# A decoder step on one core: scores before the next head's queries, sums of choices one head later, and picking and putting in an order written by hand

## Chip, cores and metric

The kernel runs on one core of a Trainium2 chip. The metric is the device time in microseconds of one execution. Before the change three runs gave a median of 2760.44 us (2749.78 to 2764.14).

The core's engines work side by side, each through its own instructions in a fixed order: PE multiplies matrices (PEld loads its weights), DVE and ACT work on vectors, POOL issues the gathers and some vector work, SP issues the plain DMAs.

## The reference, cut to what matters

The reference is one step of a hybrid decoder: a projection, a recurrent head group and an attention head group, an output projection with a layer norm, and then a mixer of experts with a second layer norm. The change touches only the mixer. For each of 256 prompt tokens and 32 sample tokens it scores 8 heads x 2 x 128 keys, takes the 16 best of each half, the 16 best sums of those, and so 128 experts of 16384 for each token; each expert is a row of `peer_u` and a row of `peer_v`, 2048 wide.

```python
def peer_ffn(x, wq, subkeys, u_tab, v_tab):
    q = (xt @ wq).reshape(n, P_HEADS, 2, P_DKEY // 2)
    s = jnp.einsum('nhcd,hckd->nhck', q, subkeys).astype(jnp.float32)
    hv, hix = lax.top_k(s, P_TOPK)
    cand = (hv[:, :, 0, :, None] + hv[:, :, 1, None, :]).reshape(n, P_HEADS, P_TOPK * P_TOPK)
    cand_e = (hix[:, :, 0, :, None] * N_KEYS + hix[:, :, 1, None, :]).reshape(n, P_HEADS, P_TOPK * P_TOPK)
    tv, tpos = lax.top_k(cand, P_TOPK)
    expert = jnp.take_along_axis(cand_e, tpos, axis=-1)
    gate = jax.nn.softmax(tv, axis=-1).astype(x.dtype)
    ...
        h = jax.nn.gelu(jnp.einsum('cd,chkd->chk', xb, u_tab[eb]), approximate=False)
        return jnp.einsum('chk,chkd->cd', gb * h, v_tab[eb])
```

## The kernel before

The text of the kernel is traced and then scheduled: a scheduler puts each engine's instructions into an order by a simulated timeline, with the place in the text as priority. So the order in the text is not the order on the engine. `tc.issue_after(ins)` puts what its block traces behind `ins` on the engine of `ins`; `tc.keep_in_program_order(ins)`, used in the change, keeps `ins` in the order of the text. Memory comes in pools (`Pool`), with `bufs` buffers in turn for each name; a tile that takes the place of an earlier one, in the same ring or in a pool that was closed, waits until the earlier one's last user is done.

The sample tokens' choices and their products with `peer_u` are done earlier, beside attention (`sample_chain`). For the 256 prompt tokens (t = 0, 1, 128 each) the mixer has four stages.

**Queries and choices** (L1698 to L1721). For each head h, two queries of 128 columns are computed from `peer_wq` (16 matmuls of 128x256 each, L1707) and copied to QP. In the next pass of the loop `choose` (L1280) scores both tokens' halves (L1286) against the keys, copies them to S (L1295, two buffers), takes 16 of 128 twice in each half on DVE (`top16`, L1272), adds 54 candidate pairs (L1306), takes 16 of these, marks their places in `hit` (L1314, DVE), multiplies by the experts' numbers (L1316, POOL), sums (L1317, DVE) and writes the row numbers to GI (L1318). Then two `dot`s follow: a dot is a gather by POOL (L422) of half an expert's row for each of 128 tokens (512 KB, tag `rows`, NRW = 4 buffers) and one DVE instruction (L1678) that multiplies it by the token's x and sums. There are 256 dots. `gates` (L1320) makes the softmax of the 128 values. All these tiles, TV with the gates' values among them, lie in pool `kq`, which closes before the next stage.

**Dense product** (L1727 to L1752). The other half of all 16384 rows of `peer_u` isn't gathered: 128 blocks of 128 rows are loaded, transposed on PE (L1735), split into a high part (ACT, L1564) and a low part (DVE `ul`, L1565), and multiplied with all tokens in three matmuls a piece (L1740); the result goes into AW (L1742), an array of 128 KB a partition that lies on memory of earlier pools. A dot or two is issued after each block, and when 128 are done, `table(0)` (L1681) transposes the row numbers, gates and dots of t = 0 into TB.

**Picking and putting** (L1765 to L1849, 64 steps of four tokens). `pick` builds one-hot marks of both halves of the expert numbers (`oo`, L1768, DVE, four buffers), transposes one half (L1772), copies it (`oT`, L1774, ACT) and multiplies with AW (`px`, L1777) to pick each token's row of products. `activate` multiplies by the other mark and sums (`xj`, L1789), adds the dots, applies gelu and the gate, and scales the marks (L1799). `put` multiplies the two marks (`pa`, L1805) and copies the result over AW (L1806): AW now holds the weights of all experts. The other dots run within the first 32 steps. Beside them `smp` (L1815) gathers the sample tokens' rows of `peer_v` (two of 512 KB for each of 32 slots, the same `rows` buffers) and adds them with eight matmul records a slot in bank fs (L1822). After the steps the sample's norm (L1862 to L1866) is done and stored.

**Last product** (L1869 to L1931). 128 blocks of 1536 columns of `peer_v` are loaded (three buffers: two in pool `vr`, one in pool `vp`), split, and multiplied with AW (L1915); the other 512 columns are gathered and added (L1890). Then the second norm.

Of the kernel before, what the change touches and what calls it, by code (L numbers as in the profile page):

```python
# [50 lines left out]
NDW = 2  # L51
# [3 lines left out]
NRW = 4  # L55
# [93 lines left out]
def hybrid_decode_step(ctx: ExitStack, tc: tile.TileContext, a, outs, dbg=None):  # L149
# [1130 lines left out]
    def choose(t, h, pool, QP, SKT, TV, tag):  # L1280


        pb = bank(tag)
        for c in range(2):
            if t < 2:
                pe.matmul(pb[:, 128 * c:128 * c + 128], QP[:, 2 * h + c, P * t:P * t + P], SKT[:, 2 * h + c, :],  # L1286
                          start=True, stop=True)
            else:
                for g in range(4):
                    k = 2 * (2 * g + h) + c  # L1290
                    pe.matmul(pb[32 * g:32 * g + 32, 128 * c:128 * c + 128], QP[:, k, :], SKT[:, k, :],
                              start=True, stop=True)
        nb_ = 2 if t < 2 else 1
        S = pool([P, 2, P], "S", bufs=nb_)
        sc.copy(S.rearrange("p a b -> p (a b)"), pb[:, :256])  # L1295
        HV, HI, HF = (pool([P, 2, 16], nm, ty, bufs=nb_) for nm, ty in (("HV", F32), ("HI", U32), ("HF", F32)))
        for c in range(2):
            top16(S[:, c, :], HV[:, c, :], HI[:, c, :])
        gp.tensor_copy(HF, HI)
        gp.tensor_scalar(HF[:, 0], HF[:, 0], 128.0, None, op0=OP.mult)  # L1300

        CV, CE = (pool([P, NCAND], nm, bufs=nb_) for nm in ("CV", "CE"))
        for dst, src, en in ((CV, HV, ve), (CE, HF, gp)):
            o = 0
            for i0, ni, w in CAND:
                en.tensor_tensor(dst[:, o:o + ni * w].rearrange("p (i j) -> p i j", i=ni),  # L1306
                                 src[:, 0, i0:i0 + ni, None].to_broadcast([P, ni, w]),
                                 src[:, 1, None, :w].to_broadcast([P, ni, w]), OP.add)
                o += ni * w
        TI, TF, EF = (pool([P, 16], nm, ty, bufs=nb_) for nm, ty in (("TI", U32), ("TF", F32), ("EF", F32)))  # L1310
        hit = pool([P, 16, NCAND], "hit", bufs=nb_)
        top16(CV, TV[:, h, :], TI)
        ve.tensor_copy(TF, TI)
        ve.tensor_tensor(hit, iota[:, None, :NCAND].to_broadcast([P, 16, NCAND]),  # L1314
                         TF[:, :, None].to_broadcast([P, 16, NCAND]), OP.is_equal)
        gp.tensor_tensor(hit, hit, CE[:, None, :].to_broadcast([P, 16, NCAND]), OP.mult)  # L1316
        ve.tensor_reduce(EF, hit, AX.X, OP.add)  # L1317
        return ve.tensor_scalar(GI[t][:, 16 * h:16 * h + 16], EF, 2.0, None, op0=OP.mult)  # L1318
# [57 lines left out]
    def sample_chain(cx):  # L1376
# [77 lines left out]
        for h in range(2):  # L1454
            choose(2, h, cx, QPs, SKT, TV, "ss")
            yield 1
# [197 lines left out]
    HD = [up([P, P], f"hd{t}") for t in range(2)]  # L1654
    dp, kq = Pool("dp", "left"), Pool("kq", "left")
    XHd, XLd = dp([P, 8, NPR], "XHd", F32R), dp([P, 8, NPR], "XLd", F32R)
    TV = [kq([P, 8, 16], f"TV{t}") for t in range(2)]
# [14 lines left out]
    def dot(n=1, upto=2 * P):  # L1672

        for i in range(got[1], min(got[1] + n, upto)):
            t, s_ = dots[i]
            fetch(min(i + NRW, upto))
            r_, h_ = rows_.pop(i), HD[t][:, s_:s_ + 1]
            ve.scalar_tensor_tensor(r_, r_, 1.0, X1a[t], op0=OP.mult, op1=OP.mult, accum_out=h_)  # L1678
            got[1] = i + 1

    def table(t):  # L1681

        pb = bank("pb")
        for q, (op_, v_) in enumerate(((OP.logical_shift_right, 8), (OP.bitwise_and, 255))):
            ii, iff = up([P, P], "ii", I32), up([P, P], "iff", bufs=2)
            ve.tensor_scalar(ii, GI[t], v_, None, op0=op_)
            if q:
                ve.tensor_scalar(iff, ii, 0.5, None, op0=OP.mult)
            else:
                ve.tensor_copy(iff, ii)  # L1690
            pe.transpose(pb[:, 128 * q:128 * q + 128], iff, ident)
# [7 lines left out]
    subkeys([kw_([P, 8, P], "wraw", bufs=WB) for _ in range(2)], SKT, "pb")  # L1699
    for h in range(9):  # L1700
        for c in (2 * h, 2 * h + 1) if h < 8 else ():
            pb = bank("pj")
            for o in range(0, 16, 8):
                w = kw_([P, 8, P], "wraw", bufs=WB)
                sy.dma_start(w, w_q[:, 128 * c:128 * c + 128].rearrange("(k p) c -> p k c", p=P)[:, o:o + 8])
                for k in range(8):
                    pe.matmul(pb[:, :NPR], w[:, k, :], XT[:, o + k, :], start=(o + k == 0), stop=(o + k == 15))  # L1707
            sc.copy(QP[:, c, :], pb[:, :NPR])
# [14 lines left out]
    banks(pt=3, ph=2, pb=3)  # L1723
    aw = Pool("aw", "right")
    AW = aw([P, 2, NPR, 64], "AW")

    def dense(i1):  # L1727
# [4 lines left out]
        for q in range(2):  # L1732
# [5 lines left out]
            for e in range(4):  # L1738
                for wi, xi in ((wh, XHd), (wh, XLd), (wl, XHd)):
                    pe.matmul(ph[:, :NPR], wi[:, e, :], xi[:, 4 * q + e, :NPR],  # L1740
                              start=(q == 0 and e == 0 and wi is wh and xi is XHd), stop=(q == 1 and e == 3 and wi is wl))
        sc.copy(AW[:, i1 // 64, :, i1 % 64], ph[:, :NPR])  # L1742
        return lo_

    tabled = []
    for i1 in range(P):
        lo_ = dense(i1)
# [3 lines left out]
        if got[1] >= P and i1 and not tabled:  # L1751
            tabled.append(table(0))  # L1752
# [10 lines left out]
    hot, prod, act = {}, {}, {}  # L1763

    def pick(u):  # L1765
        tk = slice(4 * u, 4 * u + 4)
        oo = hot[u] = x4p([P, 2, 4, P], "oo", bufs=4)
        i_ = ve.tensor_tensor(oo, iota[:, None, None, :].to_broadcast([P, 2, 4, P]),  # L1768
                              TB[:, 0:2, tk, None].to_broadcast([P, 2, 4, P]), OP.is_equal)
        pb = bank("pt")  # L1770
        for e in range(4):
            pe.transpose(pb[:, 128 * e:128 * e + 128], oo[:, 1, e, :], ident)  # L1772
        oT = x4p([P, 4, P], "oT", bufs=2)
        sc.copy(oT.rearrange("p t i -> p (t i)"), pb)  # L1774
        px = prod[u] = bank("px")
        for e in range(4):
            pe.matmul(px[:, 128 * e:128 * e + 128].rearrange("p (c j) -> p c j", c=2), oT[:, e, :], AW[:, :, 4 * u + e, :],  # L1777
                      start=True, stop=True)
        return i_

    def activate(u):

        px, o1 = prod.pop(u), hot[u][:, 0]
        if u % 2 == 0:
            act[u // 2] = x4p([P, 8], "E", bufs=2)
        E = act[u // 2]
        for e in range(4):
            xj, n_ = x4p([P, P], "xj"), 4 * (u % 2) + e
            ve.scalar_tensor_tensor(xj, px[:, 128 * e:128 * e + 128], 1.0, o1[:, e, :], op0=OP.mult, op1=OP.mult,  # L1789
                                    accum_out=E[:, n_:n_ + 1])  # L1790
        if u % 2:
            t8 = slice(4 * u - 4, 4 * u + 4)
            ve.tensor_tensor(E, E, TB[:, 3, t8], OP.add)
            sc.activation(E, E, AF.Gelu)
            ve.tensor_tensor(TB[:, 2, t8], E, TB[:, 2, t8], OP.mult)
            for v in (u - 1, u):
                for e in range(4):
                    o_ = hot[v][:, 0, e, :]
                    sc.activation(o_, o_, AF.Copy, scale=TB[:, 2, 4 * v + e:4 * v + e + 1])  # L1799

    def put(u):
        oo = hot.pop(u)
        pa = bank("pa")
        for e in range(4):
            pe.matmul(pa[:, 128 * e:128 * e + 128], oo[:, 1, e, :], oo[:, 0, e, :], start=True, stop=True)  # L1805
        sc.copy(AW[:, :, 4 * u:4 * u + 4, :], pa.rearrange("p (t c j) -> p c t j", t=4, c=2))  # L1806
# [8 lines left out]
    def smp(i):  # L1815

        s_, q = i // 2, i % 2
        sr[q] = up([P, 1024], "rows", bufs=NRW)
        gather(sr[q], vh2, ig[q][:, s_:s_ + 1])
        if q:  # L1820
            for c in range(4):
                pe.matmul(fs[32 * c:32 * c + 32, :], ws[:, s_, :], sr[c // 2][:, 512 * (c % 2):512 * (c % 2) + 512],  # L1822
                          start=(s_ == 0), stop=(s_ == 31))
# [9 lines left out]
    for s_ in range(67):  # L1833
        if s_ < 64:
            i_ = pick(s_)
        if s_ < 32:
            with tc.issue_after(i_.ins):
                dot(-(-left * (s_ + 1) // 32) + 2 * P - left - got[1])
            if s_ == 31:
                table(1)  # L1840
        if s_ < 64:
            smp(s_)
        if s_ == 40:
            rows_load(0)
            rows_load(1)
        if 0 <= s_ - 1 < 64:
            activate(s_ - 1)
        if s_ >= 3:
            put(s_ - 3)  # L1849
# [6 lines left out]
    x_, gs_, bs_ = (x4p([P, 512], nm) for nm in ("xs", "gs", "bs"))  # L1856
# [39 lines left out]
    done = 0  # L1896
    rows_load(2)
# [92 lines left out]
```

## Time and profile before

| what | value |
|---|---|
| median of three runs | 2760.44 us |
| profiled execution, its own time | 2766.85 us |
| its span | 2765.1 us |
| mean granted clock of PE | 0.915 |
| PE, DVE, ACT, POOL busy | 2415.1, 1957.2, 1044.5, 1310.3 us |

The profile is that of one execution. A row of the timeline is: start and length in us, engine, line, operation, tile written and tiles read, shape, count, and in brackets the idle time before it with what ended it. A row of groups gives line, engine, operation, names, shapes, count, then busy time, mean ns of one, then idle time of the engine just before, and what ended it. PE's matmuls are pipelined, and a matmul of full-precision numbers has more than one record, so counts of PE's rows are higher than the text's. Times of the stages are counted from the start of the span.

### The profile page before, as it was taken

The page shows a single profiled execution, that of the slowest core. Times are in us where ns is not written, and L with a number is a line of the kernel's source. Part 1 is how long each engine was busy: PE and PEld are TensorE (multiplying, and loading weights), DVE is VectorE, ACT ScalarE, POOL GpSimd, SP SyncE. Part 2 cuts the span into 40 slices and gives each one's busy share as a digit, 9 for nine tenths or more (in the row PEclk, how much of TensorE's full clock was granted, in tenths as well). Part 3 has the DMA queues.
Part 4 walks back from the last instruction along what each step waited for, and adds up shares of the span by engine and source line. Part 5 has one row for each costly group of instructions (what it writes and reads, how often), then busy time and mean ns, then how long its engine had stood idle before and what let it go on. Part 6 is the DMA issues. An engine that isn't in the chain of part 4 may idle for free. (4 is left out here: it accounts for less than half of the span.)

```text
span 2765.1 us, 47783 instructions
## 1 busy us (share of the span) xinstructions
PE 2415.1 (87%) x17636; PEld 1989.6 (72%) x17636; DVE 1957.2 (71%) x4360; ACT 1044.5 (38%) x1958; POOL 1310.3 (47%) x1348
## 2 busy tenths in 40 slices
PE   6998999799979996669499999996679799989996
PEld 4877888665656574558499999994455688878885
DVE  3699845337535367848988877886655688888988
ACT  3443224233322243231144444443334644444443
POOL 4688533214200037717544444444433077767772
PEclk9999989879879695879799999998879999999998
DMA  5788966653656757877399999997656198998895
GB/s 166 204 257 254 262 169 204 225 150 122 201 182 226 243 179 259 288 217 220 118 337 350 344 345 343 340 329 230 224 197 196 31 334 320 330 343 319 322 326 182
DMA packets 346318, 683.49 MB, mean 247 GB/s; under 512 B 81231, under 2 KB 204444, under 8 KB 345020
## 3 DMA queue, kind: packets, MB, share of 16 engines
q1 hardware_dynamic: 251172, 344.67, 38.5%
q0 software_dynamic: 94912, 335.77, 34.8%
q8 instruction: 139, 2.28, 0.3%
q14 instruction: 95, 0.77, 0.1%
HBM read 664.77 MB, written 23.88 MB: 249 GB/s over the span
## 5 line engine op out<-in xcount | busy, mean ns | idle before, releaser
L422 POOL DMA_INDIRECT rq<-in_peer_v,gi x256 | 375.4, 1466 | 219.1 <-DMA out<-xs 80.5
L422 POOL DMA_INDIRECT rows<-in_peer_u,gi x256 | 300.6, 1174 | 330.8 <-DVE rows L1678 260.4
L1678 DVE SCALAR_TENSOR_TENSOR rows<-rows,x1a 128x1024 f32<-128x1024 f32 x256 | 309.3, 1227 | 34.2 <-DMA rows<-in_peer_u,gi 30.6
L1740 PE MATMUL ph<-XHd,uh 128*128 128x256 f32 x1024 | 306.9, 300 | 0.4 <-ACT AW L1742 0.4
L1740 PE MATMUL ph<-XHd,ul 128*128 128x256 f32 x1024 | 298.9, 292 | 6.3 <-DVE ul L1565 6.0
L1740 PE MATMUL ph<-XLd,uh 128*128 128x256 f32 x1024 | 291.1, 284 | 0.0
L388 PE MATMUL pj<-XH,wl 128*128 128x288 f32 (+1 forms) x752 | 234.5, 313 | 33.8 <-POOL wl L383 17.4
L1564 ACT CAST uh<-pt 128x512 fp32r<-128x512 f32 x256 | 150.2, 587 | 275.9 <-PE ph L1740 270.6
L388 PE MATMUL pj<-XH,wh 128*128 128x288 f32 (+1 forms) x752 | 230.3, 306 | 7.0 <-DVE BV L767 4.4
L1565 DVE TENSOR_TENSOR ul<-pt,uh 128x512 fp32r<-128x512 f32 x256 | 175.6, 689 | 85.0 <-ACT uh L1564 82.1
L388 PE MATMUL pj<-XL,wh 128*128 128x288 f32 (+1 forms) x752 | 227.0, 302 | 0.0
L1915 PE MATMUL pb<-vl,ah 128*128 128x512 f32 x768 | 216.5, 391 | 2.0 <-DVE vl L1909 2.0
L1915 PE MATMUL pb<-vh,ah 128*128 128x512 f32 x768 | 197.7, 394 | 21.5 <-ACT vh L1908 21.5
L1915 PE MATMUL pb<-vh,al 128*128 128x512 f32 x768 | 215.8, 390 | 0.0
L1740 PEld LDWEIGHTS ph<-XHd,ul 128*128 128x128 f32 x1024 | 197.1, 192 | 9.5 <-DVE ul L1565 9.3
L1740 PEld LDWEIGHTS ph<-XHd,uh 128*128 128x128 f32 x1024 | 197.8, 193 | 0.7 <-ACT AW L1742 0.7
L1740 PEld LDWEIGHTS ph<-XLd,uh 128*128 128x128 f32 x1024 | 197.7, 193 | 0.0
L1890 DVE SCALAR_TENSOR_TENSOR fP<-rq,ge,fP 128x512 f32<-128x512 f32 x254 | 189.9, 748 | 6.5 <-DMA rq<-in_peer_v,gi 4.2
L381 ACT CAST wh<-wraw 128x512 fp32r<-128x512 f32 (+1 forms) x188 | 114.0, 615 | 186.5 <-PE pj L388 125.4
L1915 PEld LDWEIGHTS pb<-vh,ah 128*128 128x128 f32 x768 | 145.6, 190 | 52.2 <-ACT vh L1908 22.0
L388 PEld LDWEIGHTS pj<-XH,wl 128*128 128x128 f32 (+1 forms) x752 | 145.6, 194 | 48.8 <-DVE wl L383 22.7
L1915 PEld LDWEIGHTS pb<-vl,ah 128*128 128x128 f32 x768 | 144.7, 189 | 32.9 <-DVE vl L1909 2.9
(840 smaller groups left out, 5683.6 us busy)
## 6 DMA issues: line engine op xcount, KB each, us to landing
ur<-in_peer_u SPq DMA_DIRECT2D x128, 512.0 KB
wraw<-in_w_in SPq DMA_DIRECT2D x152, 256.0 KB
cw<-in_w_out SPq DMA_DIRECT2D x32, 512.0 KB
cw<-in_peer_wq SPq DMA_DIRECT2D x32, 512.0 KB
wraw<-in_w_out SPq DMA_DIRECT2D x32, 512.0 KB
wraw<-in_peer_wq SPq DMA_DIRECT2D x32, 512.0 KB
wraw<-in_w_in SPq DMA_DIRECT2D x64, 128.0 KB
co<-in_state_win_kv SPq DMA_DIRECT2D x16, 512.0 KB
```

The lines of the kernel that those rows point to most:

```text
L381: sc.copy(wh[:, :, :n], w[:, :, :n])
L388: pe.matmul(pb[:n, :nt], wi[:, k, :n], xi[(o + k) // 8][:, (o + k) % 8, :nt], start=(o + k == 0 and wi is wh and xi is xh), stop=(o + k == ...
L422: gp.indirect_dma_start(out=dst, out_offset=None, in_=rows_, in_offset=bass.IndirectOffsetOnAxis(ap=ix, axis=0))
L1564: sc.copy(xh, pb)
L1565: return ve.tensor_tensor(xl, pb, xh.bitcast(F32), OP.subtract)
L1678: ve.scalar_tensor_tensor(r_, r_, 1.0, X1a[t], op0=OP.mult, op1=OP.mult, accum_out=h_)
L1740: pe.matmul(ph[:, :NPR], wi[:, e, :], xi[:, 4 * q + e, :NPR], start=(q == 0 and e == 0 and wi is wh and xi is XHd), stop=(q == 1 and e == ...
L1890: ve.scalar_tensor_tensor(fP[t], r_, w_, fP[t], op0=OP.mult, op1=OP.add)
L1915: pe.matmul(acc[3 * t + q], wi[:, P * t:P * t + P], xi[:, 512 * q:512 * q + 512], start=(k == 0 and wi is ah and xi is vh), stop=(k == P - ...
```

## The change

In the queries' loop, `choose` is cut into three: `scores` (matmuls and the copy to S, now four buffers) stands in the text after the first of the next head's two queries instead of after the second; `choose` goes as far as POOL's product `hit` (four buffers); `settle`, the sum and the row numbers, stands one head later, behind the next head's `hit`. One dot follows a head instead of two, from the third pass on. TV moves from pool `kq` to `up`, and `gates` runs after `kq` is closed, with its small tile in `up`.

`table(0)` is traced once 136 dots are done, with its PE and ACT instructions behind a block's last matmul and copy.

Picking and putting becomes one loop whose instructions on PE, ACT and DVE all stay in the order of the text: pick(s), gated, put(s-4), scaled(s-3), picked(s), product_of(s-1), dots, the sample's matmuls. `oo` has six buffers, `E` three. The remaining dots run in steps 0 to 27; the sample's rows are fetched in steps 28 to 59 and added two steps later; `rows` has five buffers. `table(1)` comes at step 30. The sample's x and norm weights use `rows` buffers. Of the last product's blocks, block 0 alone is loaded ahead (at step 50 instead of two blocks at 40), into one buffer of `vr`, with two in `vp`.

```diff
-NDW = 2
+NDW = 1
-NRW = 4
+NRW = 5
...
+    def scores(t, h, pool, QP, SKT, tag):
...
+        S = pool([P, 2, P], "S", bufs=4 if t < 2 else 1)
+        sc.copy(S.rearrange("p a b -> p (a b)"), pb[:, :256])
+        return S
...
-        hit = pool([P, 16, NCAND], "hit", bufs=nb_)
+        hit = pool([P, 16, NCAND], "hit", bufs=4 if t < 2 else 1)
...
         gp.tensor_tensor(hit, hit, CE[:, None, :].to_broadcast([P, 16, NCAND]), OP.mult)
+        return i_, hit
+
+    def settle(t, h, pool, hit):
+
+        EF = pool([P, 16], "EF")
         ve.tensor_reduce(EF, hit, AX.X, OP.add)
-        return ve.tensor_scalar(GI[t][:, 16 * h:16 * h + 16], EF, 2.0, None, op0=OP.mult)
+        ve.tensor_scalar(GI[t][:, 16 * h:16 * h + 16], EF, 2.0, None, op0=OP.mult)
...
+            if h and c == 2 * h:
+                S = [scores(t, h - 1, kq, QP, SKT, "pb") for t in range(2)]
         if h:
+            late_, hits = hits, []
             for t in range(2):
-                chosen = choose(t, h - 1, kq, QP, SKT, TV[t], "pb")
-            if h > 1:
-                with tc.issue_after(chosen.ins):
-                    dot(NDW, 16 * h)
-    for t in range(2):
-        gates(t, kq, TV[t])
+                chosen, hit = choose(t, h - 1, kq, S[t], TV[t])
+                hits.append(hit)
+            with tc.issue_after(chosen.ins):
+                for t, hit in enumerate(late_):
+                    settle(t, h - 2, kq, hit)
+                if h > 2:
+                    dot(NDW, 16 * (h - 1))
+    for t, hit in enumerate(hits):
+        settle(t, 7, kq, hit)
...
+    for t in range(2):
+        gates(t, up, TV[t])
...
-        if got[1] >= P and i1 and not tabled:
-            tabled.append(table(0))
+        if got[1] >= P + 8 and not tabled:
+            with tc.issue_after(mm.ins), tc.issue_after(end.ins):
+                table(0)
+            tabled.append(0)
...
-        raw[k] = (vp if k % 3 == 2 else vr)([P, FD], "v_", bufs=1 if k % 3 == 2 else 2)
+        raw[k] = (vp if k % 3 else vr)([P, FD], "v_", bufs=2 if k % 3 else 1)
...
+    for s_ in range(68):
+        if s_ == 30:
+            table(1)
+        oT = pick(s_) if s_ < 64 else None
+        if 3 <= s_ < 66 and s_ % 2:
+            gated(s_ // 2 - 1)
+        if s_ >= 4:
+            put(s_ - 4)
+        if 0 <= s_ - 3 < 64:
+            scaled(s_ - 3)
+        if oT is not None:
+            picked(s_, oT)
+        if 0 <= s_ - 1 < 64:
+            product_of(s_ - 1)
+        if s_ < 28:
+            dot(-(-left * (s_ + 1) // 28) + 2 * P - left - got[1], keep=True)
+        elif s_ < 60:
+            smp_fetch(s_ - 28)
+        if 30 <= s_ < 62:
+            smp_add(s_ - 30)
+        if s_ == 50:
             rows_load(0)
...
-    x_, gs_, bs_ = (x4p([P, 512], nm) for nm in ("xs", "gs", "bs"))
+    r1, r2 = (up([P, 1024], "rows", bufs=NRW) for _ in range(2))
+    x_, gs_, bs_ = r1[:, :512], r1[:, 512:], r2[:, :512]
...
+    rows_load(1)
     rows_load(2)
```

`gated`, `scaled`, `product_of` and `picked` are the parts of the former `activate` and `pick`, with `pin = tc.keep_in_program_order` around each instruction.

More of the change, by code (lines that the diff above doesn't have):

```diff
@@ L1454, in sample_chain @@
         for h in range(2):
-            choose(2, h, cx, QPs, SKT, TV, "ss")
+            settle(2, h, cx, choose(2, h, cx, scores(2, h, cx, QPs, SKT, "ss"), TV)[1])
             yield 1
@@ L1699, in hybrid_decode_step @@
     subkeys([kw_([P, 8, P], "wraw", bufs=WB) for _ in range(2)], SKT, "pb")
+    hits = []
     for h in range(9):
[L1701 to L1708, printed above, removed]
+        S = []
+        for c in (2 * h, 2 * h + 1):
+            if c < 16:
+                pb = bank("pj")
+                for o in range(0, 16, 8):
+                    w = kw_([P, 8, P], "wraw", bufs=WB)
+                    sy.dma_start(w, w_q[:, 128 * c:128 * c + 128].rearrange("(k p) c -> p k c", p=P)[:, o:o + 8])
+                    for k in range(8):
+                        pe.matmul(pb[:, :NPR], w[:, k, :], XT[:, o + k, :], start=(o + k == 0), stop=(o + k == 15))
+                sc.copy(QP[:, c, :], pb[:, :NPR])
+            if h and c == 2 * h:
+                S = [scores(t, h - 1, kq, QP, SKT, "pb") for t in range(2)]
         if h:
+            late_, hits = hits, []
             for t in range(2):
[L1711 to L1716 removed]
+                chosen, hit = choose(t, h - 1, kq, S[t], TV[t])
[7 more added lines that the diff above has]
+        settle(t, 7, kq, hit)
     kw_.close()
@@ L1739, in dense @@
                 for wi, xi in ((wh, XHd), (wh, XLd), (wl, XHd)):
[L1740 to L1743, printed above, removed]
+                    mm = pe.matmul(ph[:, :NPR], wi[:, e, :], xi[:, 4 * q + e, :NPR],
+                                   start=(q == 0 and e == 0 and wi is wh and xi is XHd), stop=(q == 1 and e == 3 and wi is wl))
+        return lo_, mm, sc.copy(AW[:, i1 // 64, :, i1 % 64], ph[:, :NPR])
     tabled = []
     for i1 in range(P):
-        lo_ = dense(i1)
+        lo_, mm, end = dense(i1)
         n_ = ND + (i1 * NDN % 8 < NDN)
@@ L1813, in hybrid_decode_step, with smp_fetch, smp_add @@
     fs, sr = bank("fs"), {}
[L1815 to L1823, printed above, removed]
+    def smp_fetch(j):
+        for q in range(2):
+            sr[j, q] = up([P, 1024], "rows", bufs=NRW)
+            gather(sr[j, q], vh2, ig[q][:, j:j + 1])
+    def smp_add(j):
+        for c in range(4):
+            pin(pe.matmul(fs[32 * c:32 * c + 32, :], ws[:, j, :], sr[j, c // 2][:, 512 * (c % 2):512 * (c % 2) + 512],
+                          start=(j == 0), stop=(j == 31)))
     raw = {}
     def rows_load(k):
-        raw[k] = (vp if k % 3 == 2 else vr)([P, FD], "v_", bufs=1 if k % 3 == 2 else 2)
+        raw[k] = (vp if k % 3 else vr)([P, FD], "v_", bufs=2 if k % 3 else 1)
         sy.dma_start(raw[k], vtab[P * k:P * k + P, :FD])
     left = 2 * P - got[1]
[L1833 to L1843, printed above, removed]
-            rows_load(0)
[L1845 to L1849, printed above, removed]
+    for s_ in range(68):
[19 more added lines that the diff above has]
+        if s_ == 50:
+            rows_load(0)
     pb = bank("pb")
```

67 lines of the change are left out of this document (35 added, 32 removed).

## The prediction

> **What bounds the kernel now.** I read the busy time by stage first.
>
> ```profile
> 1190.00:1345.00 155.00, 129.22 (x622) 113.67 (x622) 105.58 (x501) 27.19 (x54) 70.95 (x126) 0.90 0.63 188
> 1345.00:1858.00 513.00, 486.89 (x4085) 483.24 (x4086) 415.68 (x728) 218.39 (x385) 237.08 (x214) 0.97 0.91 327
> 1858.00:2203.00 345.00, 260.94 (x1547) 176.48 (x1545) 221.28 (x765) 156.22 (x422) 121.14 (x111) 0.88 0.55 179
> 2203.00:2741.00 538.00, 524.74 (x2297) 433.48 (x2298) 469.79 (x454) 255.48 (x192) 375.40 (x256) 0.99 0.89 318
> ```
>
> Columns: stretch, length, busy time of PE, PEld, DVE, ACT, POOL, granted clock, DMA share, GB/s. The rows are queries and choices, dense product, picking and putting, last product. The second and fourth are full of matmuls. The third, with PE at 261 of 345 us and DVE at 221, is full of nothing: there waits bind. The joint between the first two is the other weak place. The waits show it:
>
> ```profile
> PE pt L1735 <- ACT S L1295: 13.9, 1, 13.9
> PE pb L1691 <- DVE iff L1690: 19.1, 1, 19.1
> ACT AW L1742 <- DVE ge L1328: 15.1, 1, 15.1
> ```
>
> Columns: who waited, for whom, total, times, longest. The dense product's first transposes wait 13.9 us for the last scores' copy. Then PE stands 19.1 us at table(0)'s transposes, which the order put between the first dense blocks, and ACT stands 15.1 us at its first AW copy until the last gates have run. AW cannot be written while pool kq (gates, sums, scores) is in use. ACT's timeline dates this:
>
> ```profile
> 1231.12 0.37 ACT L1708 COPY QP<-pj 128x256 f32<-128x256 f32 x1 [6.54 <-PE pj L1707]
> ...
> 1238.30 0.66 ACT L1295 COPY S<-pb 128x256 f32<-128x256 f32 x2
> ...
> 1311.60 0.82 ACT L1295 COPY S<-pb 128x256 f32<-128x256 f32 x2
> ...
> 1326.31 0.82 ACT L1295 COPY S<-pb 128x256 f32<-128x256 f32 x2
> ...
> 1377.48 1.06 ACT L1742 COPY AW<-ph 128x256 f32<-128x256 f32 x2 [15.14 <-DVE ge L1328]
> ...
> 1413.03 0.63 ACT L1742 COPY AW<-ph 128x256 f32<-128x256 f32 x1
> 1416.79 0.63 ACT L1742 COPY AW<-ph 128x256 f32<-128x256 f32 x1
> ```
>
> One dense block takes 3.75 us (1416.79 less 1413.03), and the 128 blocks in effect start at the first AW copy, 1377.5. Whatever moves that copy earlier moves all later work with it.
>
> **Part 1: choices (scores, settle, four S and hit buffers, one dot a head, gates and TV out of kq).** Moved scores issue only matmuls and copies, no DMA; settle issues none. DVE's and POOL's timelines in one head, and the group of ul subtractions:
>
> ```profile
> 1302.56 0.87 DVE L1274 MAX8 HV<-S 128x8 f32<-128x128 f32 x4
> ...
> 1309.96 2.02 DVE L1314 TENSOR_TENSOR hit<-CT,TF 128x864 f32<-128x864 f32 x2
> 1313.74 1.05 DVE L1317 TENSOR_REDUCE EF<-hit 128x16 f32<-128x864 f32 x1 [1.75 <-POOL hit L1316]
> 1314.83 0.73 DVE L1318 TENSOR_SCALAR gi<-EF 128x16 int32<-128x16 f32 x1
> ...
> 1316.65 0.17 DVE L1318 TENSOR_SCALAR gi<-EF 128x16 int32<-128x16 f32 x1
> ...
> 1319.02 0.87 DVE L1274 MAX8 HV<-S 128x8 f32<-128x128 f32 x4
> ```
>
> ```profile
> 1311.09 4.44 POOL L1316 TENSOR_TENSOR hit<-hit,CE 128x864 f32<-128x864 f32 x2
> ```
>
> ```profile
> L1565 DVE TENSOR_TENSOR ul<-pt,uh 128x512 fp32r<-128x512 f32 x256 | 175.6, 689 | 85.0 <-ACT uh L1564 82.1
> ```
>
> A head takes DVE 16.46 us (1302.56 to 1319.02): 9.4 to the end of its two hits, 7.0 after. PE delivers a head's scores every 14.7 us (1311.60 to 1326.31), so DVE falls behind and, with two S buffers, holds the last S copies, and with them PE for the 13.9 us. After the change the 7.0 becomes two reduces (2.1), two index writes (0.34 to 0.9) and one dot (1.14, rows below), with no wait for POOL: 3.6, at most 4.9 if the second index write and the dot stand behind POOL's two products, which end 3.55 us after the hits (1311.09 plus 4.44 is 1315.53). A head then costs 13.0 to 14.3, below 14.7 either way: DVE keeps up with PE. The reduce at 1313.74 ran at 1.05 beside POOL's second product, while the index write at 1314.83 took 0.73 and the next 0.17. The Trainium skill, "SBUF — State Buffer", section "Who interferes with whom", says that VectorE instructions with two SBUF inputs or in a two-port mode exclude GpSimd's reads for a whole instruction and that a reduce does not; the trace agrees, and the head would cost 14.3 by it and 13.0 without it.
>
> Scores of head 0 now follow the third query: 1231.12 plus some 1.3 for scores and copy (my estimate; two copies are 0.82) is 1232.4, 6 us before 1238.3; those of head 6, six periods of 14.7 later, are there at 1320.6. DVE: head 6 to 1334.9, choices of head 7 to 1344.3, settling of head 6 and dot to 1349.2, settling of head 7 (2.4) to 1351.6; four to six ul subtractions of the first dense blocks lie between (0.69 each, 2.8 to 4.1), and perhaps dots of the first blocks (up to 3.4). kq is free at **1355** (bounds 1350 and 1365), not 1377.5. PE has two or three blocks done by then, as before, and no table in its way: table(0) is tied behind a block's matmuls. Saved: **22.5 us**, bounds 12 and 27. The gates' ten small instructions leave this path and run beside the dense matmuls, where DVE has 97 us of 513 free; if they don't fit, under 3 us. Eight dots move from here to the picking stage, counted there; the dense stage runs 192 as before. The third buffer-saving edit (one iff) serialises two short chains, under 1 us, hidden.
>
> **Part 2: picking and putting.** Rows by third of the stage: first the oo builds alone (one a step; DVE), then the sample matmuls alone (PE, PEld), then groups, waits and landings.
>
> ```profile
> 1858.00:2060.00 202.00, 38.94 (x32) 0.82 0.68 222
> 2060.00:2130.00 70.00, 17.15 (x14) 0.97 0.73 237
> 2130.00:2192.60 62.60, 21.82 (x18) 1.00 0.00 1
> ...
> 2060.00:2130.00 70.00, 34.50 (x132) 4.62 (x132) 0.97 0.73 237
> ...
> L1678 DVE SCALAR_TENSOR_TENSOR rows<-rows,x1a 128x1024 f32<-128x1024 f32 x50 | 60.4, 1223 | 23.9 <-DMA rows<-in_peer_u,gi 20.8 <-issue 3.1
> ...
> L1793 DVE TENSOR_TENSOR E<-E,TB 128x8 f32<-128x8 f32 x32 | 5.4, 168 | 0.8
> ...
> POOL rows L422 <- PE fs L1822: 117.0, 58, 6.0
> PE fs L1822 <- DMA rows<-in_peer_v,ig: 28.9, 13, 4.7
> PE fs L1822 <- DMA rows<-in_peer_v,gi: 19.6, 8, 4.9
> ...
> DMA to landing us min/median/max: 4.0/6.4/9.7
> ```
>
> The first 32 steps take 202 us, since dots and sample rows share four buffers and one POOL queue: POOL waits for PE, PE for rows, 48.5 us of it. The next 14 steps are PE's: in 70 us stand 14 steps and 16.5 samples (132 records, eight a sample, 34.5 us busy). A sample is 2.09 and a step (70 - 34.5)/14 = 2.54. The last 18 take 3.48 each with the drain, waits between engines among it. DVE's own price of a step comes from its timeline:
>
> ```profile
> 1943.39 0.29 DVE L1789 SCALAR_TENSOR_TENSOR xj<-px,oo 128x128 f32<-128x128 f32 x1
> ...
> 1943.72 0.29 DVE L1789 SCALAR_TENSOR_TENSOR xj<-px,oo 128x128 f32<-128x128 f32 x1
> ...
> 1943.94 1.22 DVE L1768 TENSOR_TENSOR oo<-CT,TB 128x1024 f32<-128x1024 f32 x1
> 1945.08 1.22 DVE L1678 SCALAR_TENSOR_TENSOR rows<-rows,x1a 128x1024 f32<-128x1024 f32 x1
> ...
> 1946.22 1.22 DVE L1678 SCALAR_TENSOR_TENSOR rows<-rows,x1a 128x1024 f32<-128x1024 f32 x1
> ```
>
> From start to start an xj is 0.33 (four a step), oo 1.14, a dot 1.14; two small ones of 0.168 in two steps come to 0.17 a step. After the change:
> - 28 steps with 58 dots (50 and the eight): 1.32 + 1.14 + 0.17 + 2.07 x 1.14 = 4.99 on DVE, PE 2.54 beside it: 139.7.
> - Two steps with neither, at 3.48: 7.0.
> - 32 steps with one sample each: 2.54 + 2.09 = 4.63 on PE, DVE 2.6 beside it: 148.2.
> - Two more steps and the drain (the last eight scalings, two puts): four times 3.48, 14.
> - Start, and DVE's waits for rows, which were 20.8 in all: I take 7, since POOL's queue no longer holds dots' gathers behind PE (samples' gathers come after the last of them).
>
> That is 315.9 against 334.6 (1858 to 2192.6): **18.7 us** saved. Bounds: without the 7, saved 25.7; if the sample steps cost 3.48 + 2.09, as where waits between engines bind, 30 more, saved -11. The hand order's new waits: each oT copy stands before picked(s), with put(s-4) between to hide it; behind gelu on ACT stands the next oT copy, but E is ready by DVE's order before ACT has done the step's copies and scalings; six oo buffers let oo(s+1) start when put(s-5) is done, a step before. The clock in the first third is granted at 0.82; were it at half clock in all dot steps, these would be 2 x 2.54 = 5.08 on PE, 28 x 0.09 = 3 us more. The Trainium skill, "TensorE: Matmul & The Clock Gate", section "What's actually happening", gives the full clock up to an idle window of about 3.4 us; PE's idle share of a dot step here is 2.45 us, so by it the 3 us fall away.
>
> **Part 3: last product's start.** Rows at the stage's end:
>
> ```profile
> 2197.45 0.69 DVE L1366 TENSOR_TENSOR xs<-xs,bs 128x512 f32<-128x512 f32 x1
> 2204.92 0.36 SPq L1830 DMA_DIRECT2D v__23081<-in_peer_v  x1
> 2207.44 2.93 PE L1915 MATMUL pb<-vh,ah 128*128 128x512 f32 x6 [14.69 <-ACT vh L1908]
> ```
>
> The sample's norm and its 16 stores end here, PE standing 14.7. Now x, g and b go into rows buffers, free only after the last samples, six steps before the end: their 12 loads move that far back in SP's queue, where only row block 0's load stands ahead, and six steps of 3.48 cover them; and row block 1 is loaded at the stage's start. It is needed after block 0's matmuls, some 6 us after its issue, about one landing (4.0 to 9.7 for 512 KB): 0 to 3 lost. If the norm gets ahead of the last puts, up to 12 is won. I take 0, nearest to the row.
>
> **Sum.** 22.5 + 18.7 + 0 = 41.2 from the profiled execution's 2766.85 (its span is 2765.1) gives 2725.6. That execution lies 6.4 above the median 2760.44, so the forecast on the median is **2719**.
>
> **Rivals.**
> - The dense start stays stopped: the order puts another late instruction (gates, dots) ahead of the first AW copy. For it: order is the scheduler's, and it put table(0) there before. Against: table and gates are now tied or out of kq. Gain 18.7, time 2742; chance 0.13.
> - The change's pipeline doesn't run as one: steps stay at 202/32 and the rest, waits only move. For it: all engines are now bound to one order. Against: the middle third already ran at PE's price. Gain 22.5, time 2738; chance 0.14.
> - The norm gets ahead of the last puts: gain 53, time 2707; chance 0.12.
> - **Slower: the rows' round trip.** Dots cycle in five buffers, each cycle a landing plus some 0.3 of issue (estimate) and 1.14; samples are fetched two steps ahead, so two steps last at least a landing, the 0.3 and half a sample, 1.0. The samples bind from a landing of 8.0, the dots from 10.6. At 10.6 the samples cost 32 x (5.95 - 4.63) = 42 and the whole gain is gone; from there it is slower. At 12: 64 for samples and 16 for dots, time 2800. The median landing of 6.4 speaks against; chance 0.05.
> - First two together: nothing left, 2760; chance 0.04.
>
> The forecast has 0.52. **Chances** (0.5%, 14 us, is about what a measurement here can tell): faster 0.86, same 0.08, slower 0.06. The range runs from 2690, just below all three parts at their best (27 + 25.7 + 12), to 2750, which takes in the first three rivals and leaves out the last two, part 2's worst bound and whatever adds to it.
>
> **What would show it.** Right: the first AW copy at 1350 to 1365, no wait of PE for iff or S, DVE's first MAX8 at 1232; oo builds every 5.0 us through step 27 and every 4.63 from step 30; the last AW copy of putting some 316 us after the first oo. Wrong: PE waiting for rows in the sample steps above 1 us a step, DVE waiting for rows in the dot steps, AW's first copy still behind 1370, or the last product starting over 18 us after the last put.

## The result, and the profile after

Four runs of the changed kernel gave a median of 2676.97 us (2671.13 to 2701.19), four of the kernel before beside them 2762.29 (2749.78 to 2770.26): a ratio of 0.9716, with a 95% interval of 0.9655 to 0.9778. (The ratio is not that of the two medians, and it takes in a fifth run of the changed kernel, 2687.97.) The medians lie 85 us apart, about twice the 41 forecast, and below the range's 2690.

The profiled executions differ by less, 2765.1 and 2699.3 in span. The stages that the change does not touch ran 14 us longer in the profile after; in the profiles of this study the first query matmul comes between 1206 and 1223, whatever the kernel. So I count every profile from that matmul. First the stretches of the changed kernel, each row with length, busy time of PE, PEld, DVE, ACT, POOL, granted clock, DMA share and GB/s: queries and choices up to the first copy to AW, dense product up to its last copy, picking and putting, the rest.

```profile
1222.00:1379.00 157.00, 133.26 (x660) 118.17 (x660) 124.45 (x565) 17.32 (x42) 87.58 (x144) 0.92 0.60 178
1379.00:1854.00 475.00, 473.19 (x4016) 472.75 (x4016) 381.94 (x632) 214.86 (x378) 220.84 (x187) 0.99 0.94 340
1854.00:2131.00 277.00, 225.57 (x1547) 181.44 (x1545) 226.54 (x780) 156.31 (x422) 145.22 (x118) 0.87 0.69 232
2131.00:2699.00 568.00, 527.30 (x2304) 435.05 (x2304) 490.88 (x499) 261.79 (x201) 374.87 (x256) 0.97 0.86 306
```

The third row was the one full of waits: PE is busy 225.6 of 277 us now, where it was 261 of 345. Its work has become less, by 35 us, although it multiplies the same matrices. That is the surprise of this case, and the experiments are about it. The timeline of the changed kernel gives the bounds of the stretches to the hundredth:

```profile
1222.60 3.78 PE L1721 MATMUL pj<-XT,wraw 128*128 128x256 f32 x8 [0.94 <-DMA wraw<-in_peer_wq]
...
1246.55 0.66 ACT L1294 COPY S<-pb 128x256 f32<-128x256 f32 x2
...
1379.13 1.02 ACT L1764 COPY AW<-ph 128x256 f32<-128x256 f32 x2 [10.66 <-DVE gi L1327]
...
1854.28 0.61 ACT L1764 COPY AW<-ph 128x256 f32<-128x256 f32 x1 [2.33 <-PE ph L1762]
...
1855.43 1.22 DVE L1793 TENSOR_TENSOR oo<-CT,TB 128x1024 f32<-128x1024 f32 x1
...
2129.99 0.59 ACT L1836 COPY AW<-pa 128x512 f32<-128x512 f32 x1 [1.30 <-PE pa L1835]
```

And that of the kernel before, as far as it was not shown:

```profile
1208.36 3.94 PE L1707 MATMUL pj<-XT,wraw 128*128 128x256 f32 x17 [1.17 <-DMA wraw<-in_peer_wq]
...
1858.35 0.61 ACT L1742 COPY AW<-ph 128x256 f32<-128x256 f32 x1 [2.33 <-PE ph L1740]
...
2192.14 1.11 ACT L1806 COPY AW<-pa 128x512 f32<-128x512 f32 x2
```

The last row stands for two copies, the second of them at about 2192.7. I take the row's start all the same, so the third stretch before is short by some 0.6 us and the fourth long by as much. The differences of these rows:

| stretch | before | after | won | forecast |
|---|---|---|---|---|
| first query matmul to first AW copy | 169.1 | 156.5 | 12.6 | 22.5 |
| to the last dense AW copy | 480.9 | 475.1 | 5.7 | 0 |
| to the last put's AW copy | 333.8 | 275.7 | 58.1 | 18.7 |
| to the end of the span | 573.0 | 569.3 | 3.6 | 0 |
| together | 1556.7 | 1476.7 | 80.0 | 41.2 |

### The profile page after: what moved, and what is told of

Same layout as the page of the kernel before. It is cut to its first block, busy times and chain, and to the rows that moved or that the text cites. A ratio compares the mean times of both kernels' runs of the same rounds, so it can differ in the third digit from the quotient of the medians.

```text
span 2699.3 us, 47864 instructions
## 1 busy us (share of the span) xinstructions
PE 2394.6 (89%) x17636; PEld 2005.0 (74%) x17636; DVE 1962.0 (73%) x4360; ACT 1046.3 (39%) x1958; POOL 1333.8 (49%) x1348
## 4 chain that ended last, share of the span: by engine, by line
PE 61%; DVE 14%; DMA 8%; issue 5%; POOL 3%; ACT 2%; SPq 1%; DVEq 0%; POOLq 0%; ACTq 0%
PE pb L1953 19%; PE ph L1762 13%; PE pt L1757 4%; PE pj L388 3%; PE pj L1721 2%; DVE rows L1687 2%; PE pa L1601 2%; PE pa L1002 1%; PE pa L1835 1%; PE sa L881 1%; PE fs L1853 1%; PE ss L1416 1%; PE px L1805 1%; PE pa L1059 1%; DMA co<-in_cache_sel_kv,sidx 1%
## 5 line engine op out<-in xcount | busy, mean ns | idle before, releaser
L422 POOL DMA_INDIRECT rows<-in_peer_u,gi x256 | 308.4, 1205 | 320.5 <-DVE rows L1687 284.4
```

What stands on the lines that cost most here:

```text
L422: gp.indirect_dma_start(out=dst, out_offset=None, in_=rows_, in_offset=bass.IndirectOffsetOnAxis(ap=ix, axis=0))
```

## The experiments

All times are medians, beside runs of the kernel before on the same chip; "stretch" means the rows of the table above, read in each run's own profile.

**The sample's four matmuls.** Picking and putting was forecast as 32 sample steps of 4.63 us, 2.54 for the step and 2.09 for a sample. The timelines of PE show where that goes. Before (start, length, engine, line, operation, tiles, shape, records):

```profile
2094.41 1.05 PE L1822 MATMUL fs<-rows,ws 128*32 128x512 f32 x4
2095.40 0.66 PE L1772 MATMUL pt<-CT,oo 128*128 128x128 f32 x4
2095.98 1.05 PE L1822 MATMUL fs<-rows,ws 128*32 128x512 f32 x4
2096.96 0.66 PE L1772 MATMUL pt<-CT,oo 128*128 128x128 f32 x4
...
2125.19 1.06 PE L1822 MATMUL fs<-rows,ws 128*32 128x512 f32 x8
2126.18 1.37 PE L1772 MATMUL pt<-CT,oo 128*128 128x128 f32 x8
```

After:

```profile
2001.18 1.06 PE L1853 MATMUL fs<-rows,ws 128*32 128x512 f32 x8
...
2087.70 0.66 PE L1797 MATMUL pt<-CT,oo 128*128 128x128 f32 x4
2088.20 1.06 PE L1835 MATMUL pa<-oo 128*128 128x128 f32 x8
2089.09 1.16 PE L1805 MATMUL px<-AW,oT 128*128 128x128 f32 x8
2090.18 1.06 PE L1853 MATMUL fs<-rows,ws 128*32 128x512 f32 x8
2091.18 0.66 PE L1797 MATMUL pt<-CT,oo 128*128 128x128 f32 x4
...
2113.36 1.05 PE L1853 MATMUL fs<-rows,ws 128*32 128x512 f32 x4 [0.22 <-DMA rows<-in_peer_v,ig]
2114.34 0.66 PE L1797 MATMUL pt<-CT,oo 128*128 128x128 f32 x4
```

A sample has eight records, four matmuls of 512 columns that each write 32 other partitions of bank fs. Before, they stood in two pairs with other work between, and a pair of four records lasted 0.98 us from start to start (2095.98 to 2096.96), a sample so 2.0. After, all eight stand together and last 1.00 (2090.18 to 2091.18): four matmuls take as long as two. In the profile before, one sample out of 32 stood together by chance, at 2125.19: it too took 0.99. So the theory, before the runs, was that matmuls on different groups of 32 output partitions run side by side, but only while nothing else stands between them. The rival: the order by hand and the early gathers made the steps short, wherever the sample's matmuls stand. Two edits tell them apart. The first splits the four into pairs again, in the changed kernel:

```diff
+        if 30 <= s_ < 62:
+            smp_add(s_ - 30, (0, 1))
         if s_ >= 4:
             put(s_ - 4)
...
         if 30 <= s_ < 62:
-            smp_add(s_ - 30)
+            smp_add(s_ - 30, (2, 3))
```

> The changed kernel, but the four matmuls of a sample (four groups of 32 output partitions) stand in two pairs, one ahead of the put, one at the end of the step; nothing else differs. Theory (four matmuls on four column groups run side by side only where they stand back to back, a pair takes as long as all four, about 1.0 us): each of the 32 summing steps goes from 3.5 to about 4.5 us, the stretch from the last dense copy to the last put from 276 to about 307, the time about 2677 + 32 = 2709. Rival (the order written by hand and the gathers issued two steps ahead made the steps short, whatever the place of the sample's matmuls): within 5 us of 2677.

It took 2715.15 us, ratio 0.9846 (0.9744 to 0.9948); from the first query to the end 1505.7 instead of 1476.7, picking and putting 305.6 instead of 275.7. PE's timeline in this run:

```profile
2078.14 0.66 PE L1797 MATMUL pt<-CT,oo 128*128 128x128 f32 x4
2078.73 1.05 PE L1853 MATMUL fs<-rows,ws 128*32 128x512 f32 x4
2079.71 1.16 PE L1835 MATMUL pa<-oo 128*128 128x128 f32 x8
2080.70 1.06 PE L1805 MATMUL px<-AW,oT 128*128 128x128 f32 x8
2081.69 1.05 PE L1853 MATMUL fs<-rows,ws 128*32 128x512 f32 x4
2082.68 0.66 PE L1797 MATMUL pt<-CT,oo 128*128 128x128 f32 x4
```

A step is 4.54 us (2078.14 to 2082.68), within 0.1 of the 4.63 that was forecast: the forecast had the price of a sample in pairs. The theory's 2709 and 307 are met within 6 and 1.4 us; the rival's 2677 is missed by 38.

The second edit keeps them together but lets 30 of the 32 samples write the same 32 partitions with all four matmuls, so that the sampled token's sums are left out; the count, the order and the shapes stay.

```diff
-            pin(pe.matmul(fs[32 * c:32 * c + 32, :], ...
+            g_ = c if j in (0, 31) else 0
+            pin(pe.matmul(fs[32 * g_:32 * g_ + 32, :], ...
```

> The changed kernel, but for 30 of the 32 samples all four matmuls write the first 32 partitions, so the sampled token's sums are not computed. Same instructions, same order. Theory (side by side on different column groups): on one group they follow one another at about 0.98 us each where the four took 1.0, so a summing step grows by about 2.9 us, in all 30 x 2.9 = 88, time about 2765. Rival (the cost hangs on adjacency or on the count of instructions, not on the groups): within 5 us of 2677.

It took 2754.97, ratio 0.9977 (0.9945 to 1.0008), picking and putting 347.2 us. That is 71.5 more than 275.7, or 2.4 for each of the 30 samples where 2.9 was expected. PE's timeline here:

```profile
2085.42 3.62 PE L1854 MATMUL fs<-rows,ws 128*32 128x512 f32 x8
2088.97 0.66 PE L1797 MATMUL pt<-CT,oo 128*128 128x128 f32 x4
```

Four matmuls on one group last 3.55 us, 0.89 each, and I had taken a pair's 0.98 for a single one. Standing together alone does nothing; the matmuls must also write different groups of partitions. That the four here also write the same addresses is not what holds them up: the four matmuls of `pa` write different addresses, on all partitions, and take 0.99 for the same 512 columns (2079.71 to 2080.70 in the run with pairs).

Here are the rows of all 256 records, by kernel (busy time, mean ns of a record, then idle time before them): before,

```profile
L1822 PE MATMUL fs<-rows,ws 128*32 128x512 f32 x256 | 77.1, 693 | 48.5 <-DMA rows<-in_peer_v,ig 28.9 <-DMA rows<-in_peer_v,gi 19.6
```

after,

```profile
L1853 PE MATMUL fs<-rows,ws 128*32 128x512 f32 x256 | 38.4, 605 | 0.3 <-DMA rows<-in_peer_v,ig 0.2
```

in pairs,

```profile
L1853 PE MATMUL fs<-rows,ws 128*32 128x512 f32 x256 | 67.3, 605 | 0.0
```

and on one group:

```profile
L1854 PE MATMUL fs<-rows,ws 128*32 128x512 f32 x256 | 110.7, 596 | 0.0
```

The mean of one record is much the same in the last three (605, 605, 596 ns) while the busy time is 38, 67 and 111 us: busy time counts overlapping records once, the mean does not see the overlap. The first row has 77.1 where pairs alone make 67.3. The timeline of the kernel before shows where the rest lies: 16 of its pairs last longer than the others' 1.05, ten of them 1.92, and all 16 start before 2060, in the stretches with a granted clock of 0.86 (1858 to 1960) and 0.79 (1960 to 2060). That the clock is the reason was not tested.

I also tried the one edit on the kernel before, with a section of the language that keeps a block of instructions together:

```diff
+            with tc.tile_critical():
-            for c in range(4):
+                for c in range(4):
```

> The kernel before with one edit: the four matmuls of a sample always stand back to back (before, 31 of the 32 samples stand in two pairs with other work between). Theory (a sample then costs PE 1.0 instead of 2.0): in the last 32 steps, where PE sets the pace, 16.5 samples give 16 us; in the first 32, where the rows bind, little; the time about 2762 - 16 = 2746, and busy time of the 256 records falls from 77 to about 38 us. Rival (my forecast's view, a sample's matmuls cost the same wherever they stand): within 5 us of 2762, busy time 77.

2919.09 us, ratio 1.0564 (1.0525 to 1.0603): neither the theory's 2746 nor the rival's 2762. This says nothing on the question, since the edit brought waits of its own. At the section's line (L1821) the trace has 32 DRAIN instructions on the queue of PE's weight loads, mostly of 1.8 us, and semaphore waits of up to 5.0, and the waits of this run show what that does:

```profile
POOL rows L422 <- PEq L1821: 210.9, 30, 8.5
PEld fs L1823 <- issue: 165.2, 32, 9.6
```

POOL's gathers wait for PE's queue at that line 30 times, and PE's weight loads behind it stand 32 times, for nothing that the profile names. The busy time of the records did fall, from 77.1 to 57.7, at a lower granted clock (0.881 for the run).

**The two parts alone.** One run has the changed queries, choices and dense blocks with the old picking (and four row buffers), a second run the other way round:

> The changed queries, choices and dense blocks with the picking, putting and everything behind it as before (rows for four). Theory (the parts add; from the traces the choices' part is worth 18 us): about 2762 - 18 = 2744. Rival (the early start is only worth something with the new picking, because the old one gives it back in waits): within 6 us of 2762.

> The queries, choices and dense blocks as before with the changed picking, putting, norm and start of the last product (rows for five). Theory (the parts add; from the traces picking and putting with the last product's start are worth 59 + 3 us, of which some 35 are the sample's matmuls kept together): about 2700. Rival, my forecast (picking and putting worth 19 us): about 2743.

The choices alone: 2754.88, ratio 0.9981 (0.9944 to 1.0018), a gain that the times do not tell from nothing; in the profile 1545.8 us from the first query to the end, so 10.9 less than before. Picking alone: 2694.04, ratio 0.9781 (0.9693 to 0.987), 1486.4 us, so 70.3 less. The two add to 81.2, against 80.0 for both. So they add, as the theory has it, but the choices are worth 11 and not 18. Two things were booked wrongly. Picking alone has its stretch at 269.6, 6.1 shorter than in the whole change: there the eight dots that the choices hand on are missing, and the 28 dot steps, from the first oo to that of step 28, take 130.9 us instead of 136.9. And the dense stretch is 475.4 in picking alone but 483.0 in choices alone. So the 5.7 won in that stage do not come from the start or from the table, but from something in the other part, and the only thing of it that acts there is the fifth row buffer.

**Four rows instead of five** in the changed kernel:

```diff
-NRW = 5
+NRW = 4
```

> The changed kernel with row buffers for four instead of five. Theory (the fifth buffer is what shortened the dense stage, since with four DVE's dots wait for rows, the ul subtractions behind them come late and PE waits some 10 us): first to last dense copy goes from 475 to 481; in the summing steps a sample's rows wait for the sample two steps ahead, so a round trip of 6.4 plus some 0.8 us for two steps of 3.5 costs 0 to 15 more; in all 2683 to 2698. Rival (the table moved behind a block's matmuls shortened it): the dense stage stays at 475.

2705.35, ratio 0.9793 (0.9763 to 0.9823); the dense stretch is 482.0, picking and putting 290.2, each as expected (7 and 14.5 more); the time lies 7 us above the expected range. The waits of the dense stage (1400 to 1840) in this run, who for whom, total, times, longest:

```profile
PE ph L1762 <- DVE ul L1574: 4.2, 5, 1.1
DVE rows L1687 <- DMA rows<-in_peer_u,gi: 3.8, 6, 1.3
```

and in the changed kernel itself, where no dot waits for its rows in this stage:

```profile
PE ph L1762 <- DVE ul L1574: 0.9, 1, 0.9
```

A dot that waits for its rows holds DVE, the ul subtraction behind it comes late, and PE, full of matmuls, waits. PE's own waits for ul grow by 3.3 us, those of its weight loads by 4.8 (1.1 to 5.9), the stage by 7. In the sample steps (1990 to 2125 here) four rows make PE's weight loads wait for a landing:

```profile
PEld fs L1853 <- DMA rows<-in_peer_v,ig: 16.1, 19, 2.8
```

With five these waits are 3.3 us in the same steps.

**What holds the dense start.** The first AW copy came 156.5 us after the first query matmul; the forecast's 1355 was 146.6. Its row, shown with the result, waits for the last GI write. DVE's timeline of the changed kernel ahead of that:

```profile
1347.30 1.91 DVE L1687 SCALAR_TENSOR_TENSOR rows<-rows,x1a 128x1024 f32<-128x1024 f32 x1
...
1349.93 1.02 DVE L1327 TENSOR_SCALAR gi<-EF 128x16 int32<-128x16 f32 x1
...
1352.06 1.21 DVE L1687 SCALAR_TENSOR_TENSOR rows<-rows,x1a 128x1024 f32<-128x1024 f32 x1
...
1371.32 1.24 DVE L1687 SCALAR_TENSOR_TENSOR rows<-rows,x1a 128x1024 f32<-128x1024 f32 x1
...
1372.61 1.69 DVE L1327 TENSOR_SCALAR gi<-EF 128x16 int32<-128x16 f32 x1
...
1375.57 0.67 DVE L1327 TENSOR_SCALAR gi<-EF 128x16 int32<-128x16 f32 x1
...
1378.88 0.17 DVE L1327 TENSOR_SCALAR gi<-EF 128x16 int32<-128x16 f32 x1
```

Seven dots stand between head 6's choices and the last GI write, two of the heads and five of the first dense blocks. The edit makes the dots of the first five blocks, eight in all, later, one more in each block behind:

```diff
...
+        if i1 < 5:
+            owed, n_ = owed + n_, 0
+        elif owed:
+            owed, n_ = owed - 1, n_ + 1
```

> The changed kernel, but the dots of the first five dense blocks are made one a block later on. Theory (the dots that DVE makes between the last head's choices and its settling hold AW's memory, seven of them at 1.2 us, five of which go): the first AW copy comes 4 to 6 us earlier, 151 to 153 after the first query matmul instead of 156.5, the time about 2672. Rival (POOL's last products of 4.8 us or the ul subtractions hold it): the first AW copy stays within 1.5 us.

and a second one lets DVE make POOL's very last product as well:

> As the one with the dots later, and the very last hit product is made by DVE instead of POOL. Theory (with the dots gone POOL's last product is what the settling waits for; POOL takes 2.4 to 2.7 us for it and DVE about 1.0): the first AW copy another 1 to 2.5 us earlier, the time about 2670. Rival (DVE is itself the bound): no earlier, or up to 1 us later.

The first AW copy came at 151.0, 5.5 earlier, as the theory has it, but the dense stage then took 483.1: from the first query to its last copy 634.1 instead of 631.7. 2689.63 us, ratio 0.973 (0.9695 to 0.9765): no gain. With the product on DVE the copy came at 151.7, the rival's answer, time 2682.07, ratio 0.9718 (0.9682 to 0.9754). Its last GI writes took 0.16 to 0.17 each, where the run with the dots later still had one of 1.69 beside POOL's product; so that product is what made such writes long. The product took DVE 1.00 instead. From the last `hit` to the AW copy 10.2 us passed instead of 10.9, but that `hit` itself came 1.4 later; why is not shown. I thought that dots in a row were what the dense stage could not bear, and spread them, one more in every twelfth block:

> The changed kernel without the dots of the first five dense blocks (eight of them); they are made from block 9 on, one more in every twelfth block. Theory (the dots ahead of the last settling hold the first AW copy by 5.5 us, and what the run with the dots later gave back, 8 us of the dense stage, came from two or three dots a block in a row, whose rows and ul subtractions then came late): the first AW copy at 151 after the first query matmul, the dense stage at 475 to 477, so 4 to 5.5 us less in all, time about 2672. Rival (eight more dots after block 5 cost PE their time wherever they stand): the dense stage at 480 or more, time about 2677.

2686.61, ratio 0.9711 (0.9675 to 0.9747); the first copy at 151.0, the dense stage 480.2, together 631.2 against 631.7. The rival's 480 came, though spreading gave back 3 of the 8 us: eight more dots cost the dense stage 8 us in a row and 5 spread out, 0.6 each, and 5 is about what their absence ahead of it saves. How they cost it is only half seen. The waits of 1400 to 1840 have a new row in this run:

```profile
ACT AW L1764 <- PE ph L1762: 15.8, 8, 2.3
```

Eight times ACT stands at a copy to AW, with the next uh cast behind it; whether that makes the 5 us is not shown.

**A version that beats the changed kernel?** In a dot step DVE sets the pace and PE idles, so samples should be free there. Fourteen of them were moved into the dot steps, with rows in a buffer of their own (five `oo` buffers for it), the other 18 spread over the steps behind; then both edits together, and the changed kernel once more beside them. The lines that move the samples:

```diff
...
+        if s_ < 30 and s_ % 2 == 0:
+            if s_:
+                smp_add(s_ // 2 - 1)
+            if s_ < 28:
+                smp_fetch(s_ // 2)
```

> The changed kernel with 14 of the 32 samples added in the 28 dot steps (one in two steps, rows in a buffer of their own, five oo buffers instead of six for it), the other 18 spread over the 32 steps behind. Theory (a dot step is set by DVE at 4.9 and PE idles 2.4 of it, so a sample of 1.0 is free there; a step behind without one takes some 2.7 instead of 3.5): 14 x 0.8 = 11 us less, time about 2666. Rival (the dot steps are also bound by rows and DMA, so that two more rows in two steps lengthen them by 0.3 to 0.5 us): no gain or up to 10 us more.

> Both edits together: by the theories 5 + 11 = 16 us less than the changed kernel, about 2661; by the rivals 2677 to 2687.

> The changed kernel once more, on the same chip as the three before: a ratio of 0.971 to 0.973 to the kernel before, about 2677 to 2685; picking and putting at 275 to 276 and the first AW copy 156 to 157 after the first query matmul, as in its first profile.

| kernel | median | ratio to before | first query to end |
|---|---|---|---|
| samples early | 2682.47 | 0.9713 (0.9678 to 0.9748) | 1468.0 |
| early and spread | 2685.61 | 0.9713 (0.9677 to 0.975) | 1468.3 |
| changed kernel again | 2692.07 | 0.9719 (0.9677 to 0.9761) | 1474.6 |

The samples-early profile puts picking and putting at 268.0 instead of 275.3 to 275.7, 7.5 us less where 11 were expected, but the times can't tell the three apart. The changed kernel itself came out 7 us above the expected 2685 this time, 15 above its first median; its ratio and its picking and putting, 275.3, are as expected, and its first AW copy came at 155.7. The stretches of the samples-early run, dot steps and then the rest of picking:

```profile
1842.00:1978.00 136.00, 98.06 (x611) 71.83 (x611) 128.37 (x374) 60.30 (x161) 104.41 (x82) 0.89 0.90 312
1978.00:2110.00 132.00, 118.87 (x933) 94.47 (x933) 99.42 (x404) 95.28 (x260) 33.52 (x35) 1.00 0.51 164
```

and the same in the changed kernel:

```profile
1855.00:1991.00 136.00, 90.81 (x521) 83.19 (x522) 130.81 (x386) 60.80 (x161) 74.26 (x56) 0.75 0.69 226
1991.00:2131.00 140.00, 134.45 (x1025) 98.15 (x1024) 95.01 (x395) 94.91 (x260) 70.46 (x61) 0.98 0.70 239
```

PE takes more work in the first stretch and has less in the second, and the DMA share of the first goes from 0.69 to 0.90. Part of both expectations came true. From the first oo to that of step 28 the dot steps take 141.6 us instead of 136.9, so they got 4.7 longer; the steps behind them got 12.4 shorter. Whether rows or DMA lengthen the dot steps was not taken apart.

## Why the prediction was wrong, step by step

**The direction and the mechanisms of part 2 were right, its largest term was not.** The step that failed is "32 steps with one sample each: 2.54 + 2.09 = 4.63 on PE". The 2.09 was 34.5 us of busy time by 16.5 samples: a true mean, of samples that but for one stood in pairs. I carried it into an order that puts the four matmuls side by side, where a sample costs 1.0. Measured, the 32 sample steps took 113.2 us (2001.18 to 2114.34, the outer rows of PE's timeline after) instead of 148.2: 35 of the 39 us by which part 2's gain was short of the measured 58.1. With the pairs put back, the step is 4.54, so the forecast's price was right for pairs and wrong for the order that the change makes. The mean of the group hid what one row of the timeline told: the only eight records in a row, at 2125.19, took as long as four.

Of the two medians of the changed kernel, the first, 2676.97, lies below the range and the repeat, 2692.07, just inside it. The stretches settle it: 1476.7 and 1474.6 from the first query to the end in the two profiles, some 80 less than before where 41 were forecast.

The Trainium skill, "TensorE: Matmul & The Clock Gate", section "Part 3: Packing small matmuls — row/col tiling", says that matmuls at different 32-wide tile positions of the array run at the same time, the column position being set by the output's partitions. The runs agree: four take 1.00 us at four positions and 3.55 at one. That other matmuls in between end the overlap is shown by the run in pairs.

The other terms of part 2 held. Thirty steps ahead of the first sample were put at 146.7 (139.7 and 7.0) and took 145.8 (1855.4, the first oo, to 2001.2). The drain was put at 14 and took 15.6. Start and DVE's waits for rows were put at 7; the start took 1.1, and the waits lie within the 145.8. With gathers two steps ahead in five buffers, PE's matmuls waited 0.3 us for sample rows and its weight loads 3.3. The fear of the rows' round trip was sound all the same: with four buffers it cost 14.5. The clock is another matter. The forecast let the 3 us for a slower clock fall away, yet the clock granted in the dot steps was 0.75 (1855 to 1991), lower than the 0.82 before. The 3 us did not show because DVE set the pace there: 4.89 a step, against 4.99 forecast.

**Part 1** gave 12.6 at the first AW copy instead of 22.5, barely within its bounds of 12 and 27. The scores came as forecast: the first S copy 23.9 us after the first query matmul (1246.55), 6 earlier than before. What was under-sized is the clause "and perhaps dots of the first blocks (up to 3.4)". Five such dots of 1.14 stood ahead of the last GI write, 5.7 us, and the run without them moved the copy by 5.5. The rest, some 4 us, fits one dot and three GI writes that ran 0.5 to 1.5 us longer beside POOL's products, 3.6 in all, and five of the gates' small instructions on DVE that still stood ahead of the last GI write (1372.49 to 1377.51), 0.9 from start to start, where the forecast had them leave this path. That was not tested apart. The wait for S is gone, and so is PE's stop at the table. Yet the table's 19 us were not lost by themselves. Picking alone, with the table among the early blocks, has this wait in its profile and still the same dense stretch of 475.4:

```profile
PE pb L1693 <- DVE iff L1692: 17.0, 1, 17.0
```

It lies beside ACT's stop at the first AW copy, and with the table gone PE stands at AW instead:

```profile
PE ph L1762 <- ACT AW L1764: 15.9, 1, 15.9
ACT AW L1764 <- DVE gi L1327: 10.7, 1, 10.7
```

**The eight dots** handed to picking were costed there at 1.14 each, 9.1, and cost 6.1, as picking alone shows. With the choices alone the whole gain is 10.9 us. **The fifth row buffer** was costed nowhere in the dense stage and won 6 to 7 there; that this makes up for much of part 1's shortfall is luck.

**Part 3** was put at 0, and 3.6 us were won from the last put on, within its bounds of 3 lost to 12 won. PE stood 12.1 us ahead of the last product's first matmul, where it was 14.7, so most of it lies at that start; no run took it apart. Of the rivals, the slower one did not come; "the dense start stays stopped" came in part, by dots far more than by gates.

## What to carry to other kernels

Before a mean is multiplied by a count, look at single instances: a price that depends on what stands next to an instruction changes when the change reorders its neighbours. Small matmuls that write different groups of 32 output partitions belong back to back; a scheduler that fills its gaps with them in pairs pays for them twice, here 2.0 us a sample instead of 1.0. And where a stage is full, work moved into it or out of it is paid there: compare the sum of two neighbouring stages, not the joint between them.

## What the runs showed of the hardware

- Matmuls of 128x512 in full precision with 32 output partitions: one after another on one group 0.89 us each (3.55 for four), two on two groups 0.98, four on four groups 1.00. So four groups give 3.5 times the pace of one.
- Between the two widths of matmul no stop can be seen in the run in pairs: a step with the sample in two places takes 4.54, and its parts from start to start (0.59, 0.98, 0.99, 0.99, 0.99) leave no gap.
- On DVE a write of 128x16 row numbers took 0.17 us alone, and 0.67 to 1.69 while POOL ran its product; a dot 1.91 instead of 1.21.
